# A transformer block on one core: stationary operands of the 256-column products moved by 64 bytes

## The chip, the core and the metric

The kernel runs on one core of one Trainium2 chip. The metric is the device time of one execution in microseconds; the kernel before has three such times. One further execution was recorded by the hardware profiler, and every row shown here is from that one.

On a core, PE (TensorE) multiplies: a *stationary* operand of 128 columns is loaded into the array by a weight load (PEld in the profile), then a *moving* operand of up to 512 columns is streamed past it. Both are read from the on-chip memory SBUF, and the product is written to a PSUM bank. DVE (VectorE) and ACT (ScalarE) do elementwise work, POOL (GpSimd) a little of it, and SP issues most of the transfers from main memory.

## The reference

One block over 512 tokens of width 1024, with a memory of 256 tokens:

```python
def reference(x, mem, ...):
    mix = hybrid_mixer(x, ...)                    # 4 gated-recurrence heads, 4 mLSTM heads
    x = layer_norm(ALPHA * x + mix, ln1_g, ln1_b)
    ca = memory_cross_attention(x, mem, ca_wq, ca_wkv, ca_wo)
    x = layer_norm(ALPHA * x + ca, ln2_g, ln2_b)
    ff = conv_ffn(x, ffn_w_up, ffn_conv_w, ffn_conv_b, ffn_w_down)
    return layer_norm(ALPHA * x + ff, ln3_g, ln3_b)

def memory_cross_attention(x, mem, wq, wkv, wo):
    q = (x @ wq).reshape(bsz, s, CA_HEADS, CA_DH)           # 512 tokens, 4 heads of 256
    k, v = jnp.split(mem @ wkv, 2, axis=-1)                 # 256 memory tokens
    sc = einsum('bshd,bmhd->bhsm', q, k) * CA_DH ** -0.5
    o = einsum('bhsm,bmhd->bshd', softmax(sc), v).reshape(bsz, s, d)
    return o @ wo

def conv_ffn(x, w_up, conv_w, conv_b, w_down):              # 1024 -> 2 x 2816 -> 1024
    gate, val = jnp.split(causal_dwconv(x @ w_up, conv_w, conv_b), 2, axis=-1)
    return (gelu(gate) * val) @ w_down
```

All arrays are float32.

## The kernel before

**Products.** Every float32 operand of a large product is kept as two parts of type fp32r: a rounded part (names ending in h) and the rest (names ending in l). ACT makes the first by a cast, DVE the second by a subtraction: `split` (lines 124 and 125) for weights, `split_evict` (lines 243 and 244) for results that leave PSUM. `mm3` (lines 154 to 156) then issues three products for one: high by high, high by low, low by high. Its first argument after the PSUM bank is the high part of the stationary operand, and each of the three products has a weight load of its own.

**Two shapes of loop.** `col_tile` takes a weight block of 128 columns as stationary operand and streams activations past it. `slab` takes 128 tokens of activations as stationary operand and streams 512 columns of weights. Most products therefore have 512 moving columns. Those with 256 are: the keys (`col_units` over `ca_wkv`, 8 units, the memory's 256 tokens moving), the first two units of the up-projection (`up_units`, computed in two halves of 256 tokens so that the first half can start before the last layer-normalized block is there), the scores in `attend` (queries stationary, keys moving), the products with the values in `pv` (values stationary, probabilities moving), and the last token block of the down-projection, which `slab` cuts into two halves of 256 weight columns (`halves=True`).

**Where operands lie.** Pools hand out buffers per tag, in rotation. Weights come from main memory into `raw` (three buffers of 8192 bytes in each partition), their parts go to `wh` and `wl` (four buffers of 4096 bytes each). Large activations have tag X (`X8`, ten buffers of 8192 bytes); later ones have tag H in a pool that comes after. Small unused tiles (`WP_PAD` and its like) fill up the pools in front. In the built program each buffer of `raw`, `wh`, `wl`, X and H begins at a multiple of 128 bytes within the partition, the slices that products take from them are 512 bytes or a multiple of that apart, and so every fp32r operand of a product begins at a multiple of 128 bytes. The first `wh` buffer lies 256 bytes past a multiple of 512, and the X buffers at multiples of 512. An operand that begins elsewhere is `vaug` (64 bytes past a multiple of 128, and from there in steps of 4 bytes from head to head), a moving operand of float32 products.

**Order.** The engines run their instructions in the order in which they were issued, and the planner of the language has laid out that order from the program text (only the first stage is written by hand). PE goes through the stages one after the other; transposes (lines 252, 417 and 748) stand between the products where their inputs were expected to be ready.

Of the kernel before, what the change touches and what calls it, by code (L numbers as in the profile page):

```python
# [10 lines left out]
F32R = mybir.dt.float32r  # L11
# [6 lines left out]
P = 128  # L18
# [3 lines left out]
KT = D // P  # L22
# [7 lines left out]
QSCALE = P ** -0.5  # L30
CSCALE = 256 ** -0.5
WARM = 7

HEAD = ((0, 1), (1, 1), (2, 2), (4, 2), (6, 2))
CONST_PAD, WP_PAD, SM_PAD = 40, 64, 16
# [4 lines left out]
def hybrid_block_kernel(  # L40
# [28 lines left out]
    wp = ctx.enter_context(tc.tile_pool(name="wp", bufs=1))  # L69
    xp = ctx.enter_context(tc.tile_pool(name="xp", bufs=1))  # L70
# [4 lines left out]
    def mm_bank():  # L75
        return pm.tile([P, 512], F32, name="mm", tag="mm", bufs=5)

    def mx_bank():
        return pm.tile([P, 512], F32, name="mx", tag="mx", bufs=3)

    def X8(dt, name):
        return xp.tile([P, 2048], dt, name=name, tag="X", bufs=10)

    def small(n, name, bufs=4):
        return sm.tile([P, n], F32, name=name, tag=name, bufs=bufs)
# [10 lines left out]
    def f32(t):  # L96
        return t.bitcast(F32)
# [12 lines left out]
    def load_raw(src_list, shape):  # L110
        r = wp.tile([P, 2048], F32, name="raw", tag="raw", bufs=3)
        a, c = shape
        rv = r.rearrange("p (a c) -> p a c", a=a)
        for dst, src in src_list(rv):
            nc.sync.dma_start(dst, src)
        return rv

    def split(src, shape):
        h = wp.tile([P, 1024], F32R, name="wh", tag="wh", bufs=4)
        l = wp.tile([P, 1024], F32R, name="wl", tag="wl", bufs=4)  # L120
        a, c = shape
        hv = h.rearrange("p (a c) -> p a c", a=a)
        lv = l.rearrange("p (a c) -> p a c", a=a)
        A.copy(hv, src)  # L124
        V.tensor_sub(lv, src, f32(hv))  # L125
        return hv, lv

    def slab_units(w, c0, nk):

        k, per = 0, 4  # L130
        while k < nk:
            n = min(4, nk - k)
            raw = load_raw(
                lambda rv, k=k, n=n: [(rv[:, j:min(j + per, n), :],
                                       w[(k + j) * P:(k + min(j + per, n)) * P, c0:c0 + 512]
                                       .rearrange("(k p) c -> p k c", p=P)) for j in range(0, n, per)],
                (4, 512))
            for u in range(0, n, 2):
                h, l = split(raw[:, u:u + 2, :], (2, 512))
                yield k + u, 2, h, l  # L140
            k += n

    def col_units(w, c0, n):

        for j in range(0, n, 2):
            raw = load_raw(
                lambda rv, j=j: [(rv, w[:, c0 + j * P:c0 + (j + 2) * P]
                                  .rearrange("(k p) c -> p k c", p=P))], (8, 256))
            for i in range(2):
                h, l = split(raw[:, :, i * P:(i + 1) * P], (8, P))  # L150
                yield j + i, h, l

    def mm3(ps, ah, al, bh, bl, first, last):
        T.matmul(ps, ah, bh, start=first, stop=False, skip_group_check=True)  # L154
        T.matmul(ps, ah, bl, start=False, stop=False, skip_group_check=True)  # L155
        T.matmul(ps, al, bh, start=False, stop=last, skip_group_check=True)  # L156
# [41 lines left out]
    def col_tile(ps, h, l, xh, xl):  # L198
        for k in range(KT):
            mm3(ps, h[:, k, :], l[:, k, :], xh(k), xl(k), k == 0, k == KT - 1)  # L200
# [7 lines left out]
    wps = mx_bank()  # L208
    for _ in range(WARM):
        T.matmul(wps[:, 0:P], warm, warm, start=True, stop=True)  # L210
# [31 lines left out]
    def split_evict(ps, h, l):  # L242
        A.copy(h, ps)
        V.tensor_sub(l, ps, f32(h))
# [14 lines left out]
    def kslice(ts_, k, c0=0, n=S):  # L259
        o = (k % 4) * 512 + c0  # L260
        return ts_[k // 4][:, o:o + n]

    xTh = [X8(F32R, "xTh") for _ in range(2)]
    xTl = [X8(F32R, "xTl") for _ in range(2)]
    tok = lambda ts_: (lambda k, b: kslice(ts_, k, b * P, P))
    feat = lambda ts_: (lambda k: kslice(ts_, k))
# [4 lines left out]

    binb = q1p.tile([P, 512], F32, name="binb", tag="binb", bufs=2)
    hv = X8(F32, "hv").rearrange("p (b c) -> p b c", b=NB)
    ps = [mm_bank() for _ in range(NB)]

    with tc.manual_schedule(engines={mybir.EngineType.PE, mybir.EngineType.Activation, mybir.EngineType.DVE}):
        for (k0, n), xr, wr in zip(HEAD, xraw, raw0):
            h = wp.tile([P, 1024], F32R, name="wh", tag="wh", bufs=4).rearrange("p (a c) -> p a c", a=2)
            l = wp.tile([P, 1024], F32R, name="wl", tag="wl", bufs=4).rearrange("p (a c) -> p a c", a=2)
            xk = lambda ts_: ts_[k0 // 4].rearrange("p (a c) -> p a c", a=4)[:, k0 % 4:k0 % 4 + n, :]  # L280
            A.copy(h[:, 0:n, :], wr[:, 0:n, :])
            V.tensor_copy(xk(xTh), xr[:, 0:n, :])  # L282
            V.tensor_sub(l[:, 0:n, :], wr[:, 0:n, :], f32(h[:, 0:n, :]))  # L283
            V.tensor_sub(xk(xTl), xr[:, 0:n, :], f32(xk(xTh)))  # L284
            for b in range(NB):
                for i in range(n):
                    k = k0 + i
                    mm3(ps[b], kslice(xTh, k, b * P, P), kslice(xTl, k, b * P, P), h[:, i, :], l[:, i, :],
                        k == 0, k == KT - 1)
# [29 lines left out]

    wif = wp.tile([P, KT, 8], F32, name="wif")  # L320
    nc.sync.dma_start(wif, w_in0[:, MI:MI + 8].rearrange("(k p) c -> p k c", p=P))
    wifh = wp.tile([P, 1024], F32R, name="wh", tag="wh", bufs=4).rearrange("p (k c) -> p k c", k=KT)
    G.memset(f32(wifh), 0.0)
    for j in range(2):
        src = wif[:, :, 4 * j:4 * j + 4]
# [56 lines left out]
    for i, h, l in col_units(w_in0, HF, 4):  # L382
        ps = mm_bank()
        col_tile(ps, h, l, feat(xTh), feat(xTl))
        lf, kin = tt("lf"), tt("kin")
        A.activation(lf, ps, AF.Sigmoid, bias=col(BIN + 4 + i))
        A.activation(kin, ps, AF.Sigmoid, bias=nbin[:, 4 + i:5 + i], scale=-1.0)
        V.tensor_scalar(kin, kin, oml[:, i:i + 1], None, op0=OP.mult)
        lfs[i], kins[i] = lf, kin
    qs = {}  # L390
    for i, h, l in col_units(w_in0, HQ, 4):
        ps = mm_bank()
        col_tile(ps, h, l, feat(xTh), feat(xTl))
        q = tt("q")
        A.activation(q, ps, AF.Sigmoid, bias=col(BIN + i))
        V.scalar_tensor_tensor(q, ps, col(BIN + i), q, op0=OP.add, op1=OP.mult)
        qs[i] = q
# [142 lines left out]
    for base, sc in ((MK, 1.0), (MQ, QSCALE)):  # L540
        for i, h, l in col_units(w_in0, base, 4):
            ps = mm_bank()
            col_tile(ps, h, l, feat(xTh), feat(xTl))
            kq[base, i] = conv_silu(ps, i + (4 if base == MK else 0), sc)
# [78 lines left out]
    mtok = lambda t: (lambda k, b: t[:, k * 256 + b * P:k * 256 + (b + 1) * P])  # L623
    wkv = ca_wkv[0]
    kmh, kml = X8(F32R, "kmh"), X8(F32R, "kml")
    for i, h, l in col_units(wkv, 0, KT):
        if i % 2 == 0:
            ps = mm_bank()
        col_tile(ps[:, (i % 2) * 256:(i % 2 + 1) * 256], h, l, mcols(mTh), mcols(mTl))
        if i % 2 == 1:  # L630
            s = slice((i - 1) * 256, (i + 1) * 256)
            split_evict(ps, kmh[:, s], kml[:, s])
# [63 lines left out]
    x1_last = slab(tok(yTh), tok(yTl), w_out[0], 512, KT, ln1_evict, late=4)  # L696


    vmh, vml = (X8(F32R, n).rearrange("p (b c) -> p b c", b=2) for n in ("vmh", "vml"))

    def v_slab(j, mid=None):
        slab(mtok(mTh), mtok(mTl), wkv, D + j * 512, KT,
# [3 lines left out]
    v_slab(0, x1_last)  # L706


    qmh = [X8(F32R, "qmh") for _ in range(2)]
    qml = [X8(F32R, "qml") for _ in range(2)]  # L710
    for i, h, l in col_units(ca_wq[0], 0, KT):
        ps = mm_bank()
        col_tile(ps, h, l, feat(x1h), feat(x1l))
# [90 lines left out]
        A.copy(kslice(hTh, i), g)  # L804
        V.tensor_sub(kslice(hTl, i), g, f32(kslice(hTh, i)))

    def up_units(i):
        raw = load_raw(lambda rv: [(rv[:, :, j * P:(j + 1) * P],
                                    ffn_w_up[0][:, j * DFF + i * P:j * DFF + (i + 1) * P]
                                    .rearrange("(k p) c -> p k c", p=P)) for j in range(2)], (8, 256))  # L810
        return [split(raw[:, :, j * P:(j + 1) * P], (8, P)) for j in range(2)]

    early = 2
    units = [up_units(i) for i in range(early)]
    banks = [[mm_bank(), mm_bank()] for i in range(early)]
    for half in range(2):
        c0 = half * 256
        for i in range(early):
            for j in range(2):
                if (half, i, j) == (0, 1, 1):  # L820
                    x2_last()
                h, l = units[i][j]
# [31 lines left out]
def build(shapes):  # L854
    import concourse.bacc as _bacc

    nc = _bacc.Bacc("TRN2", target_bir_lowering=False, num_devices=1, dynamic_dma_scratch_size=1024)
    args = [nc.dram_tensor(f"in_{n}_dram", shapes[n], F32, kind="ExternalInput").ap() for n in _INS]
    args.append(nc.dram_tensor("out_0_dram", (1, S, D), F32, kind="ExternalOutput").ap())
    with tile.TileContext(nc) as tc:  # L860
        hybrid_block_kernel(tc, *args)
    return nc
# [19 lines left out]
```

## Time and profile before

| | |
|---|---|
| three executions | 819.33, 821.69 and 823.42 us, median 821.69 |
| the profiled execution's own time | 819.77 us |
| its span, first to last instruction | 818.1 us |
| PE busy | 801.5 us, 98% of the span |
| weight loads (PEld) busy | 674.0 us, 82% |
| DVE, ACT busy | 504.9 us (62%), 318.8 us (39%) |
| granted TensorE clock, mean | 0.995 of full |

In a page row such as `L154 PE MATMUL mm<-x2h,wh 128*128 128x512 f32`, the first name after the arrow is the moving operand and the second the stationary one; 128*128 is the stationary shape, 128x512 the product. The duration of a product is not what it costs in a stream, since products overlap in the array; what one costs is the distance from its start to the next one's. A weight load for the next product runs under the current one.

### The profile page before, as it was taken

The page shows a single profiled execution, that of the slowest core. Times are in us where ns is not written, and L with a number is a line of the kernel's source. Part 1 is how long each engine was busy: PE and PEld are TensorE (multiplying, and loading weights), DVE is VectorE, ACT ScalarE, POOL GpSimd, SP SyncE. Part 2 cuts the span into 40 slices and gives each one's busy share as a digit, 9 for nine tenths or more (in the row PEclk, how much of TensorE's full clock was granted, in tenths as well). Part 3 has the DMA queues.
Part 4 walks back from the last instruction along what each step waited for, and adds up shares of the span by engine and source line. Part 5 has one row for each costly group of instructions (what it writes and reads, how often), then busy time and mean ns, then how long its engine had stood idle before and what let it go on. Part 6 is the DMA issues. An engine that isn't in the chain of part 4 may idle for free.

```text
span 818.1 us, 10034 instructions
## 1 busy us (share of the span) xinstructions
PE 801.5 (98%) x4000; PEld 674.0 (82%) x4000; DVE 504.9 (62%) x863; ACT 318.8 (39%) x434; POOL 30.2 (4%) x52
## 2 busy tenths in 40 slices
PE   8989999999999999999999999999999999999996
PEld 6868887777789888888988988888888888888885
DVE  6563397899787488348548676665566556224237
ACT  3289553353344225237413354444444444222110
POOL 2000100100200010000001000000000000000001
PEclk9999999999999999999999999999999999999998
DMA  8726423135119316321311552223333322142102
GB/s 268 199 72 184 119 79 55 52 81 177 65 52 340 124 52 224 106 84 52 102 58 47 156 154 82 87 89 103 103 104 103 103 99 77 57 154 82 48 1 103
DMA packets 86263, 87.86 MB, mean 107 GB/s; under 512 B 3140, under 2 KB 65732, under 8 KB 86216
## 3 DMA queue, kind: packets, MB, share of 16 engines
q1 hardware_dynamic: 85632, 84.58, 33.6%
q10 hardware_dynamic: 584, 2.64, 0.9%
q8 instruction: 31, 0.51, 0.2%
q14 instruction: 16, 0.13, 0.1%
HBM read 85.10 MB, written 2.12 MB: 107 GB/s over the span
## 4 chain that ended last, share of the span: by engine, by line
PE 88%; DVE 5%; DMA 4%; POOL 1%; issue 1%; ACT 0%; SPq 0%; DVEq 0%; ACTq 0%; POOLq 0%
PE mm L154 27%; PE mm L155 27%; PE mm L156 27%; DMA raw<-in_w_in_dram 3%; PE mx L574 1%; DMA binb<-in_b_in_dram 1%; PE mx L586 1%; PE mx L252 1%; PE mx L464 1%; POOL ss L423 1%; DMA raw<-in_x_t_dram 1%; PE mx L465 1%; PE mx L154 0%; DVE wl L125 0%; PE mx L156 0%
## 5 line engine op out<-in xcount | busy, mean ns | idle before, releaser
L125 DVE TENSOR_TENSOR wl<-raw,wh 128x1024 fp32r<-128x1024 f32 x134 | 163.2, 1221 | 230.3 <-ACT wh L124 229.7
L124 ACT CAST wh<-raw 128x1024 fp32r<-128x1024 f32 x134 | 140.7, 1052 | 242.8 <-PE mm L156 133.0
L154 PE MATMUL mm<-x2h,wh 128*128 128x512 f32 (+1 forms) x384 | 142.8, 372 | 0.0
L155 PE MATMUL mm<-x2l,wh 128*128 128x512 f32 (+1 forms) x384 | 142.6, 371 | 0.0
L156 PE MATMUL mm<-x2h,wl 128*128 128x512 f32 (+1 forms) x384 | 142.6, 371 | 0.0
L155 PEld LDWEIGHTS mm<-x2l,wh 128*128 128x128 f32 x384 | 72.4, 188 | 12.5
L156 PEld LDWEIGHTS mm<-x2h,wl 128*128 128x128 f32 x384 | 72.4, 188 | 12.5
L154 PEld LDWEIGHTS mm<-x2h,wh 128*128 128x128 f32 x384 | 72.4, 188 | 12.3
L155 PE MATMUL mm<-wl,hTh 128*128 128x512 f32 (+1 forms) x198 | 72.4, 366 | 0.0
L154 PE MATMUL mm<-wh,hTh 128*128 128x512 f32 (+1 forms) x198 | 72.4, 366 | 0.0
L795 DVE SCALAR_TENSOR_TENSOR fc<-mm,cols,fc 128x511 f32<-128x511 f32 x88 | 65.6, 746 | 1.5
L156 PE MATMUL mm<-wh,hTl 128*128 128x512 f32 (+1 forms) x180 | 65.8, 365 | 0.0
L154 PE MATMUL mm<-wh,xTh 128*128 128x512 f32 x128 | 51.5, 402 | 0.8 <-DVE xTh L282 0.8
L155 PE MATMUL mm<-wl,xTh 128*128 128x512 f32 x128 | 51.2, 400 | 0.6 <-DVE wl L283 0.5
L156 PE MATMUL mm<-wh,xTl 128*128 128x512 f32 x128 | 50.8, 397 | 0.7 <-DVE xTl L284 0.6
L156 PE MATMUL mm<-xTh,wl 128*128 128x512 f32 x128 | 51.1, 399 | 0.0
L154 PE MATMUL mm<-xTh,wh 128*128 128x512 f32 x128 | 51.1, 399 | 0.0
L155 PE MATMUL mm<-xTl,wh 128*128 128x512 f32 x128 | 51.0, 398 | 0.0
L154 PEld LDWEIGHTS mm<-wh,hTh 128*128 128x128 f32 x198 | 37.4, 189 | 6.2
L155 PEld LDWEIGHTS mm<-wl,hTh 128*128 128x128 f32 x198 | 37.4, 189 | 6.1
L156 PEld LDWEIGHTS mm<-wh,hTl 128*128 128x128 f32 x180 | 33.9, 189 | 5.4
L804 ACT CAST hTh<-fc 128x512 fp32r<-128x512 f32 x22 | 13.7, 620 | 55.7 <-DVE fc L803 55.7
(265 smaller groups left out, 1387.9 us busy)
## 6 DMA issues: line engine op xcount, KB each, us to landing
raw<-in_ffn_w_up_dram SPq DMA_DIRECT2D x44, 512.0 KB, 4.8
raw<-in_w_in_dram SPq DMA_DIRECT2D x14, 1024.0 KB, 8.5
raw<-in_ffn_w_down_dram SPq DMA_DIRECT2D x10, 1024.0 KB, 4.8
raw<-in_ca_wkv_dram SPq DMA_DIRECT2D x8, 1024.0 KB, 5.9
raw<-in_w_out_dram SPq DMA_DIRECT2D x4, 1024.0 KB, 8.8
raw<-in_ca_wq_dram SPq DMA_DIRECT2D x4, 1024.0 KB, 5.4
raw<-in_ca_wo_dram SPq DMA_DIRECT2D x4, 1024.0 KB, 4.9
wt<-scr ACTq DMA_DIRECT2D x4, 640.0 KB, 4.0
```

The lines of the kernel that those rows point to most:

```text
L124: A.copy(hv, src)
L125: V.tensor_sub(lv, src, f32(hv))
L154: T.matmul(ps, ah, bh, start=first, stop=False, skip_group_check=True)
L155: T.matmul(ps, ah, bl, start=False, stop=False, skip_group_check=True)
L156: T.matmul(ps, al, bh, start=False, stop=last, skip_group_check=True)
L252: T.transpose(ps[:, i * P:(i + 1) * P], src[:, k * P:(k + 1) * P], ident)
L423: G.tensor_tensor(out_, out_, neghalf[:, 0:n], op=OP.pow)
L464: T.matmul(at[:, s], ke[:, s], qe[:, s], start=True, stop=True, skip_group_check=True)
L465: T.matmul(at[0:CH, b * P + CH:(b + 1) * P], kxe[:, b, :], qbo[:, b, :], start=True, stop=True, skip_group_check=True)
L574: T.matmul(ps[:, 0:LEN[j]], kT_[:, j * P:(j + 1) * P], qT_[:, j * P:], start=True, stop=True)
L795: V.scalar_tensor_tensor(y[:, s:], ps[:, :S - s], col(FCW + (2 - s) * 44 + ft), y[:, s:], op0=OP.mult, op1=OP.add)
L804: A.copy(kslice(hTh, i), g)
```

## The change

The stationary operands of four of the five groups of 256-column products are moved by 16 elements, that is 64 bytes: the weights of the keys, the weights of the first two up-projection units, the queries and the values. To make room, each buffer of `wh` and `wl` becomes 32 elements (128 bytes) longer and so does each X buffer, whether its tile is moved or not. Tiles that are not moved take the buffer's first elements. The fifth group, the halved last block of the down-projection, has stationary operands that 512-column products use as well; they stay where they are.

```diff
+SKEW = 16
...
-    def X8(dt, name):
-        return xp.tile([P, 2048], dt, name=name, tag="X", bufs=10)
+
+    def X8(dt, name, skew=0):
+        return xp.tile([P, 2080], dt, name=name, tag="X", bufs=10)[:, skew:skew + 2048]
...
-    def split(src, shape):
-        h = wp.tile([P, 1024], F32R, name="wh", tag="wh", bufs=4)
-        l = wp.tile([P, 1024], F32R, name="wl", tag="wl", bufs=4)
+    def split(src, shape, skew=0):
+        h = wp.tile([P, 1056], F32R, name="wh", tag="wh", bufs=4)[:, skew:skew + 1024]
+        l = wp.tile([P, 1056], F32R, name="wl", tag="wl", bufs=4)[:, skew:skew + 1024]
...
-    def col_units(w, c0, n):
+    def col_units(w, c0, n, skew=0):
...
-                h, l = split(raw[:, :, i * P:(i + 1) * P], (8, P))
+                h, l = split(raw[:, :, i * P:(i + 1) * P], (8, P), skew)
...
-    for i, h, l in col_units(wkv, 0, KT):
+    for i, h, l in col_units(wkv, 0, KT, SKEW):
...
-    vmh, vml = (X8(F32R, n).rearrange("p (b c) -> p b c", b=2) for n in ("vmh", "vml"))
+    vmh, vml = (X8(F32R, n, SKEW).rearrange("p (b c) -> p b c", b=2) for n in ("vmh", "vml"))
...
-    qmh = [X8(F32R, "qmh") for _ in range(2)]
-    qml = [X8(F32R, "qml") for _ in range(2)]
+    qmh = [X8(F32R, "qmh", SKEW) for _ in range(2)]
+    qml = [X8(F32R, "qml", SKEW) for _ in range(2)]
...
-    def up_units(i):
+    def up_units(i, skew=0):
...
-        return [split(raw[:, :, j * P:(j + 1) * P], (8, P)) for j in range(2)]
+        return [split(raw[:, :, j * P:(j + 1) * P], (8, P), skew) for j in range(2)]
...
-    units = [up_units(i) for i in range(early)]
+    units = [up_units(i, SKEW) for i in range(early)]
```

Two places that took 1024-element buffers of `wh` and `wl` directly (the hand-ordered first stage and the gates' weights) take the first 1024 of the 1056.

## Rows read from the trace of the kernel before

**Rows 1.** The page: busy time, granted clock in 40 slices, chain that ended last.

```profile
PE 801.5 (98%) x4000; PEld 674.0 (82%) x4000; DVE 504.9 (62%) x863; ACT 318.8 (39%) x434; POOL 30.2 (4%) x52
...
PEclk9999999999999999999999999999999999999998
...
PE 88%; DVE 5%; DMA 4%; POOL 1%; issue 1%; ACT 0%; SPq 0%; DVEq 0%; ACTq 0%; POOLq 0%
```

**Rows 2.** Groups by shape, PE: 256-column products; count, busy us, mean ns.

```profile
L154 PE MATMUL mm<-mTh,wh 128*128 128x256 f32 x64 | 18.7, 292 | 0.0
...
L154 PE MATMUL mm<-x2h,wh 128*128 128x256 f32 x64 | 18.3, 285 | 0.0
...
L155 PE MATMUL mm<-wl,hTh 128*128 128x256 f32 x44 | 12.4, 283 | 0.0
...
L154 PE MATMUL mm<-kmh,qmh 128*128 128x256 f32 x32 | 9.2, 288 | 0.0
...
L154 PE MATMUL mx<-pth,vmh 128*128 128x256 f32 x32 | 9.1, 285 | 0.1
```

**Rows 3.** Timeline of PE, second half of the first up-projection units; start, duration.

```profile
458.28 0.28 PE L155 MATMUL mm<-x2l,wh 128*128 128x256 f32 x1
...
458.87 0.28 PE L154 MATMUL mm<-x2h,wh 128*128 128x256 f32 x1
...
459.35 0.28 PE L155 MATMUL mm<-x2l,wh 128*128 128x256 f32 x1
...
472.43 0.28 PE L156 MATMUL mm<-x2h,wl 128*128 128x256 f32 x1
```

**Rows 4.** Timeline of the weight loads in the same stretch.

```profile
459.35 0.19 PEld L156 LDWEIGHTS mm<-x2h,wl 128*128 128x128 f32 x1
459.47 0.19 PEld L154 LDWEIGHTS mm<-x2h,wh 128*128 128x128 f32 x1
```

**Rows 5.** Windows: 256 columns, then the other up-projection units at 512.

```profile
459.35:472.55 13.20, 13.20 (x113) 13.20 (x111) 7.54 (x10) 7.38 (x9) 0.00 (x0) 1.00 0.41 135
472.55:690.17 217.62, 217.62 (x962) 180.25 (x961) 134.85 (x163) 94.84 (x123) 0.00 (x0) 1.00 0.33 99
```

**Rows 6.** Groups by shape, weight loads: count, busy us, mean ns.

```profile
L154 PEld LDWEIGHTS mm<-mTh,wh 128*128 128x128 f32 x64 | 12.3, 192 | 0.0
...
L154 PEld LDWEIGHTS mm<-x1h,wh 128*128 128x128 f32 x64 | 12.0, 188 | 2.5
...
L464 PEld LDWEIGHTS mx<-ee 128*128 128x128 f32 x32 | 5.0, 188 | 1.6 <-DVE ee L442 0.5
...
L465 PEld LDWEIGHTS mx<-xo 128*64 128x64 f32 x32 | 3.1, 134 | 2.1 <-issue 0.2
```

**Rows 7.** The chain in order of time: eight transposes; four float32 passes.

```profile
378.74 0.87 PE mx L748 x8
...
118.41 0.45 PE mx L489 x4
```

**Rows 8.** Line 124, ACT's cast of weights: what its idle time waited for (us, times).

```profile
  PE mm L156: 133.0, 42
  PE mm L155: 79.7, 63
```

**Rows 9.** Timelines around the last transposes of the second layer normalization.

```profile
455.86 1.40 DVE L673 SCALAR_TENSOR_TENSOR xres<-xres,lnrs,lnb 128x512 f32<-128x512 f32 x2
...
457.29 1.04 PE L252 MATMUL mx<-ident,xres 128*128 128x128 f32 x8
```

**Rows 10.** Timelines of PE and DVE in the products with the values.

```profile
391.94 0.28 PE L156 MATMUL mx<-pth,vml 128*128 128x256 f32 x1
392.29 0.36 PE L154 MATMUL mx<-pth,vmh 128*128 128x256 f32 x1
...
391.72 0.76 DVE L244 TENSOR_TENSOR ptl<-mx,pth 128x256 fp32r<-128x256 f32 x2 [0.62 <-ACT pth L243]
```

**Rows 11.** Lines 523 and 404, DVE's writes: duration ns min/median/max.

```profile
L523 DVE TENSOR_TENSOR vaug<-mm,binb x4: 669/676/680, 140.5 to 144.6; 128x512 f32<-128x512 f32 x4
...
L404 DVE TENSOR_TENSOR hgu<-mm,binb x4: 680/682/691, 101.3 to 106.8; 128x512 f32<-128x512 f32 x4
```

More of the change, by code (lines that the diff above doesn't have):

```diff
@@ L277, in hybrid_block_kernel @@
         for (k0, n), xr, wr in zip(HEAD, xraw, raw0):
-            h = wp.tile([P, 1024], F32R, name="wh", tag="wh", bufs=4).rearrange("p (a c) -> p a c", a=2)
-            l = wp.tile([P, 1024], F32R, name="wl", tag="wl", bufs=4).rearrange("p (a c) -> p a c", a=2)
+            h = wp.tile([P, 1056], F32R, name="wh", tag="wh", bufs=4)[:, 0:1024].rearrange("p (a c) -> p a c", a=2)
+            l = wp.tile([P, 1056], F32R, name="wl", tag="wl", bufs=4)[:, 0:1024].rearrange("p (a c) -> p a c", a=2)
             xk = lambda ts_: ts_[k0 // 4].rearrange("p (a c) -> p a c", a=4)[:, k0 % 4:k0 % 4 + n, :]
@@ L321, in hybrid_block_kernel @@
     nc.sync.dma_start(wif, w_in0[:, MI:MI + 8].rearrange("(k p) c -> p k c", p=P))
-    wifh = wp.tile([P, 1024], F32R, name="wh", tag="wh", bufs=4).rearrange("p (k c) -> p k c", k=KT)
+    wifh = wp.tile([P, 1056], F32R, name="wh", tag="wh", bufs=4)[:, 0:1024].rearrange("p (k c) -> p k c", k=KT)
     G.memset(f32(wifh), 0.0)
```

## The prediction

> **What bounds the kernel now.** I read the page first. PE is busy for 98% of the span, holds 88% of the chain that ended last, and the granted clock is at its upper level, 2.4 GHz, throughout [rows 1]. So time saved on PE is time saved, unless another engine is only just ahead of it.
>
> Next the groups by shape, to count what the change touches [rows 2]. The row shown for each group is one of mm3's three lines. Keys: 3 x 64 = 192 products; first up-projection units: 192; scores: 3 x 32 = 96; products with the values: 96. That is 576 products. The halves of the last down-projection block, with hTh stationary, also have 256 columns, and are not moved: they are the control.
>
> Then the timelines, for the distance from start to start. From 459.35 to 472.43 us there are 109 products, so one costs 13.08 / 109 = 0.120 us [rows 3]. In the 512-column stretch, 960 products share 217.62 us, 226.7 ns each [rows 5]. The difference between the two shapes is 106.7 ns for 256 more columns, which is 2.4 columns a ns: at that clock a column a cycle. So streaming costs 106.7 and 213.3 ns, and both shapes pay 13.3 ns on top. The change can only pay through these 13.3 ns, or add to them.
>
> What are they? The weight load of the next product starts with each product, at 459.35 beside a product at 459.35 [rows 3, 4]. With 256 columns the load takes up the whole distance: PEld is busy 13.20 of 13.20 us, while with 512 it has 17% of the time free [rows 5]. Two rows hint that the two reads of SBUF disturb each other. The loads under 256-column keys last 192 ns on average and those under 512-column products 188 [rows 6]. And the same up-projection product, with the same operands, costs 118 ns in the first five distances after a pause (458.28 to 458.87) and 120 later, with nothing waited for [rows 3]. A fixed price of the instruction would not change like that.
>
> **The change part by part.** *Instructions.* None is added, removed or reordered in the text. Each product, load, cast and subtraction has the same shape as before; only start addresses differ, and the pools grow by 8 x 128 + 10 x 128 = 2304 bytes a partition. Transfers land in raw, which is neither longer nor moved. *The casts and subtractions that write the moved tiles.* I price them at nothing: DVE wrote vaug, whose rows begin 64 bytes off and in steps of 4 bytes, in 676 ns, and an operation of the same shape into an aligned tile took 682 [rows 11]. ACT has no such row; were its casts slower, they would be hidden, as ACT's idle time before them is spent on waiting for PE to release buffers, 133.0 + 79.7 us [rows 8]. *The moved stationary operands.* No row shows an fp32r stationary operand anywhere but at a multiple of 128 bytes, so the price has to be bounded.
>
> Lower bound of the cost: eight transposes, each with a full load of 128 columns, follow each other in 0.87 us, 109 ns each, and four float32 passes in 0.45 us, 112 ns each [rows 7]. So loads of that size can be had every 109 ns. If the move undid all disturbance, a 256-column product would cost 109: 120 - 109 = 11 ns x 576 = 6.3 us saved. Upper bound: if a shifted row made the load read 64 bytes, that is 16 columns, more. A load of 64 columns lasts 134 ns, one of 128 columns 188 [rows 6], so a column costs 54 / 64 = 0.84 ns and 16 of them 13.5 ns; loads are end to end here, so all of it shows: 13.5 x 576 = 7.8 us lost. Between lies nothing, 0.
>
> I take a partial gain. The row of the same product at 118 and the two rows at 109 and 112 are all below 120, and none with 256 columns in a steady stream is above; the middle of 118 and 109 is 113.5, so 6.5 ns x 576 = 3.7 us.
>
> Two rules of the Trainium skill speak against any gain. The page TensorE: Matmul & The Clock Gate (section Step-by-step: what each phase is for) says that the loads have a read port of their own, so that loading the next operand takes nothing from the running product. The page SBUF — State Buffer (section Specifications (TRN2)) puts the memory's lines at 16 bytes, and a shift of 64 is a whole number of these, so that a load would touch as many lines as before. By either, the sum would be 0 instead of -3.7 us. The loads of 192 and 188 ns are the only thing in the trace that speaks against the first; no row bears on the second.
>
> *What is given back.* Where PE already runs level with another engine, a faster product only waits. At 457.29 PE begins the transposes of the last normalized block, and DVE ends that block's normalization at 455.86 + 1.40 = 457.26 [rows 9]. Ahead of them stand 72 moved products, which would end 72 x 6.5 = 0.47 us earlier. The second four transposes need DVE's last piece and would stand at 457.29 + 0.44 - 0.47 = 457.26: nothing is lost at 6.5 ns, and 0.3 us at 11. In the products with the values PE starts at 392.29, 0.23 us later than the 120 after 391.94 would make it, upon DVE's piece of ptl [rows 10]; the scores' 96 x 6.5 = 0.6 us could be lost to that, if DVE's chain does not move along. I take 0.5 us in all, and 0.9 at 11 ns. Likeliest sum: -3.7 + 0.5 = -3.2 us.
>
> *The longer buffers.* The 512-column products, some 2,900, are not moved, but distances between their operands change by multiples of 128 bytes. I price this at nothing: scores, with both operands in X (a multiple of 512 apart), and keys, with wh and X (256 past one), both run at 120. A distance of 128 has no row. One ns each way would be 2.9 us, so the range leaves some room for it.
>
> **The rivals.**
>
> *Part of the overhead goes* (forecast): the profiled execution's 819.77 becomes 816.6. That execution was 1.9 us below the median of the three runs, 821.69; against the median it is 818.5 us.
>
> *All of it goes*: 109 ns. 576 x 11 = 6.3, less 0.9: -5.4, so 816.3 us. For it: rows 7. Against: those rows are float32 passes with 128 moving columns, not fp32r at a column a cycle; and the 512-column products, whose loads end long before they do, pay 13.3 ns as well.
>
> *The move does nothing.* The 13.3 ns are the same for both shapes, to the tenth, as if they belonged to the fp32r product and not to the load. Then the time is 821.7. Against: the 118 ns after a pause. The Trainium skill's rule of a separate read port for loads (TensorE: Matmul & The Clock Gate, Step-by-step: what each phase is for) would give this too, by way of reads that never meet; it has this rival's chance.
>
> *The load becomes longer*, and the kernel slower: a stationary row that begins in the middle of a 128-byte stretch costs the load 13.5 ns. It decides as soon as a load needs more than 120 ns from start to start, which is where the 256-column stages already stand [rows 5]. Price +7.8 us, 829.5. Against it stands only that DVE does not mind such rows [rows 11]; PE has none.
>
> **How the numbers follow.** Chances: part of it goes 0.34, all 0.21, nothing 0.28, longer load 0.17. The least that a measurement of this kernel can tell from no change is about 0.5%, 4.1 us. All (5.4 us) is beyond that, and a quarter of the partial cases, those under 112 ns: 0.21 + 0.09 = 0.30 faster. Slower: the longer load but for small sizes of it, 0.15. Same: 0.55. Predicted: 818.5 us. The range reaches from 813.0 (all of it, with a run 2.4 below the median as the lowest of the three was, and some room for the 512-column products) to 824.0 (nothing, with a run like the highest of three, 823.4). That leaves out the longer load and little else, under 2 in 10.
>
> **What would show each step.** In the timeline of the first up-projection units after the change: distances of 109 to 118 ns, loads near 188 instead of 192. The control should still stand at 120 and the 512-column stretch at 226.7. At the transposes after the first 72 products a pause of up to 0.3 us, before the values' second unit one of up to 0.8. Distances of 133 would show the longer load, 120 that nothing moved. The prediction is wrong in kind if the 512-column products change, since then buffer length and not the 64 bytes sets the time, and wrong in size if the four groups do not gain alike.

## The result and the profile after

The changed kernel takes 829.45 us (median of 5 runs, 829.12 to 831.0); the kernel before, on the same chip, 820.36 (5 runs, 819.33 to 823.42). The ratio is 1.0107, with an interval of 1.0084 to 1.0129. The change makes the kernel slower, outside the predicted range. The profiled execution is the slowest of the five, 831.0 us with a span of 829.3: 11.2 more than before (the medians are 9.1 apart).

First the page of the kernel after: busy time, granted clock in 40 slices, chain that ended last. Line numbers are two higher than before, so mm3's three lines are L156 to L158.

```profile
PE 812.4 (98%) x4000; PEld 673.7 (81%) x4000; DVE 505.2 (61%) x863; ACT 318.8 (38%) x434; POOL 30.2 (4%) x52
...
PEclk9999999999999999999999999999999999999998
...
PE 89%; DMA 5%; DVE 4%; POOL 1%; issue 1%; ACT 0%; SPq 0%; DVEq 0%; ACTq 0%; POOLq 0%
```

Against [rows 1] one figure moved: PE is busy 10.9 us longer with the same 4000 matmuls, and that is nearly the span's 11.2. The clock is at the same level, and PEld, DVE and ACT are busy within 0.3 us of before. So nothing new is waited for: products themselves cost more.

Which ones is read from windows of the kernel after (start and end; length; busy time and instructions of PE, PEld, DVE, ACT, POOL; granted clock; DMA share; GB/s). In order of time: the last 96 key products; the 192 query products, which have 512 columns; the last 48 products with the values; 119 products of the first up-projection units' second half; 960 products of the other units, with 512 columns.

```profile
core 0: us, PE busy (x) PEld busy (x) DVE busy (x) ACT busy (x) POOL busy (x), PEclk, DMA share, GB/s
253.98:264.86 10.88, 10.88 (x98) 10.88 (x97) 7.35 (x8) 5.19 (x6) 0.00 (x0) 1.00 1.01 358
323.84:368.48 44.64, 44.64 (x193) 36.19 (x192) 16.37 (x19) 12.32 (x17) 0.00 (x0) 1.00 0.39 136
401.14:406.60 5.46, 5.46 (x51) 5.46 (x49) 2.67 (x5) 2.36 (x4) 0.00 (x0) 1.00 0.65 187
463.05:477.06 14.01, 14.01 (x121) 14.01 (x120) 8.24 (x11) 8.00 (x11) 0.00 (x0) 1.00 0.44 143
477.06:699.74 222.68, 222.68 (x962) 180.56 (x961) 134.95 (x163) 94.93 (x123) 0.00 (x0) 1.00 0.32 97
```

Divide each length by its products. Keys: 10.88 / 96 = 113.3 ns where they had 120. Values: 5.46 / 48 = 113.7. First up-projection units: 14.01 / 119 = 117.7. These are the moved ones and they gained. The stretch of [rows 5], which the change does not mention, has gone from 226.7 to 222.68 / 960 = 232.0 ns, with the clock at 1.00 and every engine's load in it as before. The query products, also unmoved, went from 226.7 (43.52 us for 192 before) to 44.64 / 192 = 232.5.

The weight loads of the kernel after, by shape (count, busy us, mean ns, idle before), answer to [rows 6]:

```profile
L156 PEld LDWEIGHTS mm<-mTh,wh 128*128 128x128 f32 x64 | 12.1, 189 | 0.0
...
L156 PEld LDWEIGHTS mm<-x1h,wh 128*128 128x128 f32 x64 | 12.2, 190 | 2.9
...
L156 PEld LDWEIGHTS mm<-x2h,wh 128*128 128x128 f32 x384 | 72.4, 188 | 14.0
```

Under the keys 192 became 189, and under the query products 188 became 190. The up-projection's loads (the last line; most of them lie under 512 columns) last 188 ns, though its products became 5.3 ns dearer. No load became 13.5 ns longer.

Last the timeline of PE after, in the keys, at the values' second unit and at the transposes:

```profile
253.98 0.28 PE L156 MATMUL mm<-mTh,wh 128*128 128x256 f32 x1
254.10 0.28 PE L157 MATMUL mm<-mTl,wh 128*128 128x256 f32 x1
254.21 0.28 PE L158 MATMUL mm<-mTh,wl 128*128 128x256 f32 x1
...
396.40 0.28 PE L158 MATMUL mx<-pth,vml 128*128 128x256 f32 x1
396.72 0.36 PE L156 MATMUL mx<-pth,vmh 128*128 128x256 f32 x1
...
461.94 0.28 PE L158 MATMUL mm<-x2h,wl 128*128 128x256 f32 x1
462.06 1.04 PE L254 MATMUL mx<-ident,xres 128*128 128x128 f32 x8
```

Starts are 0.11 to 0.12 us apart in the keys. The pause before the values' second unit is 0.32 - 0.12 = 0.20 us, before it was 0.23 [rows 10]. At the transposes there is none: 0.12 us after the last product.

**The account.** The mean distance from start to start (pauses left out) was taken from both timelines for each group of products, and its change multiplied by the group's count. With 512 columns: the mixer's first products 768 x 3.1 = 2.4 us, its output 192 x 4.4 = 0.85, values' projection 96 x 2.8 = 0.27, queries 192 x 5.8 = 1.1, cross-attention's output 192 x 3.9 = 0.75, up-projection 960 x 5.3 = 5.1, down-projection 462 x 4.0 = 1.85: together +12.3 us. With 256 columns: keys 192 x 5.9 = 1.1, first up-projection units 192 x 2 = 0.4, values 0.2, halved last block 0.2: -1.9. The net, 10.4, is most of the span's 11.2.

### The profile page after: what moved, and what is told of

The parts are those of the page before. It is cut to its first block, busy times and chain, and to the rows that moved or that the text cites. A ratio compares the mean times of both kernels' runs of the same rounds, so it can differ in the third digit from the quotient of the medians.

```text
span 829.3 us, 10034 instructions
## 1 busy us (share of the span) xinstructions
PE 812.4 (98%) x4000; PEld 673.7 (81%) x4000; DVE 505.2 (61%) x863; ACT 318.8 (38%) x434; POOL 30.2 (4%) x52
## 4 chain that ended last, share of the span: by engine, by line
PE 89%; DMA 5%; DVE 4%; POOL 1%; issue 1%; ACT 0%; SPq 0%; DVEq 0%; ACTq 0%; POOLq 0%
PE mm L156 27%; PE mm L157 27%; PE mm L158 27%; DMA raw<-in_w_in_dram 3%; PE mx L576 1%; DMA binb<-in_b_in_dram 1%; PE mx L588 1%; PE mx L254 1%; PE mx L466 1%; POOL ss L425 1%; DMA raw<-in_x_t_dram 1%; PE mx L467 0%; DVE wl L127 0%; PE mx L156 0%; PE mx L419 0%
## 5 line engine op out<-in xcount | busy, mean ns | idle before, releaser
L158 PE MATMUL mm<-x2h,wl 128*128 128x512 f32 (+1 forms) x384 | 144.2, 375 | 0.0
L156 PE MATMUL mm<-x2h,wh 128*128 128x512 f32 (+1 forms) x384 | 144.1, 375 | 0.0
L156 PEld LDWEIGHTS mm<-x2h,wh 128*128 128x128 f32 x384 | 72.4, 188 | 14.0
L158 PEld LDWEIGHTS mm<-x2h,wl 128*128 128x128 f32 x384 | 72.1, 188 | 14.0
L156 PE MATMUL mm<-wh,hTh 128*128 128x512 f32 (+1 forms) x198 | 73.0, 369 | 0.0
L158 PE MATMUL mm<-wh,hTl 128*128 128x512 f32 (+1 forms) x180 | 66.1, 367 | 0.0
L156 PE MATMUL mm<-wh,xTh 128*128 128x512 f32 x128 | 52.5, 410 | 0.8 <-DVE xTh L284 0.8
L158 PE MATMUL mm<-wh,xTl 128*128 128x512 f32 x128 | 51.6, 403 | 0.3 <-DVE xTl L286 0.3
L156 PE MATMUL mm<-xTh,wh 128*128 128x512 f32 x128 | 51.4, 402 | 0.0
L158 PE MATMUL mm<-xTh,wl 128*128 128x512 f32 x128 | 51.1, 399 | 0.0
L156 PEld LDWEIGHTS mm<-wh,hTh 128*128 128x128 f32 x198 | 37.2, 188 | 6.7
L158 PEld LDWEIGHTS mm<-wh,hTl 128*128 128x128 f32 x180 | 33.8, 188 | 6.2
## 6 DMA issues: line engine op xcount, KB each, us to landing
raw<-in_w_out_dram SPq DMA_DIRECT2D x4, 1024.0 KB, 10.4
```

## The experiments

**The question.** The unmoved products share only one thing with the edit: their operands lie in buffers that became 128 bytes longer. Each next `wh` and `wl` buffer, and each next X buffer, therefore starts 128 bytes further along modulo 256, and the distance between a stationary and a moving operand, which was a multiple of 256, becomes in the built program an odd multiple of 128 for about half of the unmoved products. The theory: that distance sets what a product costs beyond its columns. The rivals: the 64-byte move itself slows what comes after; it is the buffers' absolute place; or it is the change from one product's operands to the next one's.

**The length without the move.**

```diff
-SKEW = 16
+SKEW = 0
```

> The buffers are longer by 128 bytes as in the changed kernel, but nothing is moved by 64. Theory A (the buffer length, by which starts no longer agree modulo 256, slows the 512-column products): the 512-column up-projection stays at about 232 ns a product, keys go back to 118 to 120; time 830 to 833 us. Rival B (the 64-byte move itself costs, by its loads or by what follows them): 512 columns back at 226.7, keys at 120, time 820.4.

Measured: 831.2 us, ratio 1.0125 (1.0097 to 1.0153). Windows of the last 96 keys and of the 960 up-projection products:

```profile
254.12:265.51 11.39, 11.39 (x98) 11.39 (x97) 7.25 (x8) 5.17 (x6) 0.00 (x0) 1.00 0.98 371
...
477.85:700.53 222.68, 222.68 (x963) 180.72 (x961) 134.98 (x163) 94.68 (x123) 0.00 (x0) 1.00 0.32 97
```

The 960 products take 222.68 us, to the hundredth what they take in the kernel after, with nothing moved by 64 bytes. So the length alone makes the loss. The keys without the move cost 11.39 / 96 = 118.6 ns, so 5.3 of their 6.7 ns came with the move.

**Half of the lengths each.** In the first, X buffers go back to 2048 elements, with queries and values not moved (the upper part of the diff); in the second, `wh` and `wl` go back to 1024, with keys and first up-projection weights not moved (the lower part; the line of `wl` is like that of `wh`).

```diff
-        return xp.tile([P, 2080], dt, name=name, tag="X", bufs=10)[:, skew:skew + 2048]
+        return xp.tile([P, 2048], dt, name=name, tag="X", bufs=10)[:, skew:skew + 2048]
...
-        h = wp.tile([P, 1056], F32R, name="wh", tag="wh", bufs=4)[:, skew:skew + 1024]
+        h = wp.tile([P, 1024], F32R, name="wh", tag="wh", bufs=4)[:, skew:skew + 1024]
```

> Only the weight buffers wh and wl are 128 bytes longer, keys and first up-projection weights are moved by 64; the X buffers have their old length, queries and values are not moved. A: some of the slowing stays (one operand of each 512-column product changes its place modulo 256 from buffer to buffer): 228 to 232 ns, 824 to 830 us; keys near 113. B: 512 columns at 226.7 and only the keys and first up-projection units slower than 120.

> Only the X buffers are 128 bytes longer, queries and values are moved by 64; wh and wl as before. A: 228 to 232 ns with 512 columns, 824 to 830 us; keys at 118 to 120. B: 512 columns at 226.7, scores and products with the values slower than 120. If the weight buffers alone cause it, this one is at 226.7 and 819 us.

Measured: 830.03 us, 1.011 (1.0087 to 1.0133), with longer weight buffers; 827.4 us, 1.0082 (1.006 to 1.0105), with longer X buffers. Windows of the queries and the 960 up-projection products, longer weight buffers first:

```profile
323.84:368.49 44.65, 44.65 (x194) 36.20 (x192) 16.37 (x19) 12.30 (x17) 0.00 (x0) 1.00 0.39 134
476.65:699.86 223.21, 223.21 (x962) 181.09 (x961) 135.20 (x163) 94.94 (x123) 0.00 (x0) 1.00 0.33 97
```

```profile
322.51:366.02 43.51, 43.51 (x193) 36.05 (x192) 16.45 (x19) 12.30 (x17) 0.00 (x0) 1.00 0.40 137
473.89:696.82 222.93, 222.93 (x962) 180.63 (x961) 134.93 (x163) 94.69 (x123) 0.00 (x0) 1.00 0.32 97
```

Either half alone makes most of the loss, and the losses do not add up, as they would if each buffer had a price of its own. The queries tell the halves apart: their activations (x1h, x1l) lie in H buffers, which nothing lengthened, so only the weight buffers' length can change the distance, and only then do they cost 232.6 instead of 226.6 ns. In the up-projection the activations (x2h, x2l) lie in X, and both lengths count.

**Lengths that keep the distance.** The same move of 64 bytes in buffers longer by 512 bytes (weights alone, then X alone: the two parts of the diff) and by 256 bytes (weights alone, 1088 elements); what is not lengthened is not moved. Where X grows, the unused tile `WP_PAD` goes, and `warm` takes part of `cols`, to make room.

```diff
-        h = wp.tile([P, 1056], F32R, name="wh", tag="wh", bufs=4)[:, skew:skew + 1024]
+        h = wp.tile([P, 1152], F32R, name="wh", tag="wh", bufs=4)[:, skew:skew + 1024]
...
-        return xp.tile([P, 2080], dt, name=name, tag="X", bufs=10)[:, skew:skew + 2048]
+        return xp.tile([P, 2176], dt, name=name, tag="X", bufs=10)[:, skew:skew + 2048]
```

> Keys and first up-projection weights are moved by 64, but wh and wl are 512 bytes longer, so that every unmoved start is where it was modulo 512; X as before. A: 512 columns back at 226.7; keys and the first up-projection units at 113.3: 384 x 6.7 = 2.6 us saved, less up to 0.5 given back: 817.8 to 818.5 us, faster than before. B: slower than before, 821 to 826 us. A third case, that any move of the later pools slows the 512-column products: 232 ns, 830 us.

> Queries and values moved by 64, X buffers 512 bytes longer; wh and wl as before, keys and up-projection weights not moved (for room, the warm-up products at the start read the columns tile instead of one of their own, and the pad tile of the weight pool is gone). 512 columns at 226.7, keys and first up-projection units at 120; scores and products with the values near 113, that is 192 x 6.5 = 1.2 us less, of which up to 0.6 is given back where PE waits for the softmax: 819.0 to 820.0 us.

> Keys and first up-projection weights moved by 64 with wh and wl 256 bytes longer (128 in the change, 512 in the run that restored the 512-column products). If 128-odd starts alone cost: 512 columns at 226.7, 819 us. If a step of 256 from one load to the next costs too, as single rows of the run with weights 128 bytes longer hint (230 ns where the next start is 256 away): 227 to 229 ns on average, 820 to 824 us.

Measured: 819.21 us, 0.9988 (0.9976 to 1.0001); 818.62 us, 0.9987 (0.997 to 1.0003); 819.13 us, 0.9986 (0.9971 to 1.0). Windows of the last 96 keys (weights by 512) or 48 values (X by 512) and of the 960 up-projection products:

```profile
253.46:264.34 10.88, 10.88 (x98) 10.88 (x97) 7.35 (x8) 5.17 (x6) 0.00 (x0) 1.00 1.02 380
...
474.10:691.73 217.63, 217.63 (x963) 180.31 (x961) 134.98 (x163) 94.75 (x123) 0.00 (x0) 1.00 0.33 99
```

```profile
396.10:401.54 5.44, 5.44 (x50) 5.44 (x49) 2.77 (x5) 2.36 (x4) 0.00 (x0) 1.00 0.66 191
...
471.65:689.27 217.62, 217.62 (x962) 180.25 (x961) 134.88 (x163) 94.84 (x123) 0.00 (x0) 1.00 0.33 99
```

The move keeps its gain (10.88 / 96 and 5.44 / 48 are both 113.3 ns), and the 512-column products are back at 217.63 / 960 = 226.7. With 256 bytes the up-projection is at 226.7 too, and the keys at 11.30 / 96 = 117.7:

```profile
249.69:260.99 11.30, 11.30 (x98) 11.30 (x97) 7.27 (x8) 5.16 (x6) 0.00 (x0) 1.00 1.02 371
470.69:688.32 217.63, 217.63 (x963) 180.25 (x961) 134.99 (x163) 94.89 (x123) 0.00 (x0) 1.00 0.33 99
```

The gain is read from the stages. None of the three ratios is clear of no change, though the first run was expected to be faster, at 817.8 to 818.5 us.

**A constant distance.** Here and in the next experiment the kernel before is edited. A small tile in front of `wh` shifts all weight buffers by 64 or by 128 bytes, and one behind them fills the shift up to 512 bytes, so that buffer lengths stay and all that comes behind keeps its place modulo 512.

```diff
+    wp.tile([P, 16], F32, name="shift_pad")     # 32 for 128 bytes
...
+    wp.tile([P, 112], F32, name="rest_pad")     # 96 for 128 bytes
```

> The kernel before, but all wh and wl buffers together begin 64 bytes later, at the old distance of 4096 from each other: every product with weights now has one operand 64 bytes past a multiple of 128, the 512-column ones too. No buffer is longer. Theory A in the form 'a constant offset of 64 helps, changing offsets hurt': keys and first up-projection units 113 to 118 ns, 512 columns at or below 226.7, 814 to 819 us. In the form '64 helps 256-column products and hurts those of 512': 512 columns at 230 to 236, 828 to 845 us.

> As the run with all weights 64 bytes later, but 128 bytes: the distance between the two operands of a product is an odd multiple of 128, the same for all weight buffers. If the offset of 128 itself is what costs, the 512-column products stand at 233 to 235 ns throughout, 838 to 843 us. If only the change of offset from buffer to buffer costs, they stand at 226.7 and the time is that of before, 820.

Measured: 831.04 us, 1.0141 (1.0118 to 1.0164), and 833.08 us, 1.0161 (1.0134 to 1.0187). Windows of the last 96 keys and the 960 up-projection products, 64 bytes first (there also the first 282 products of the down-projection):

```profile
252.60:263.48 10.88, 10.88 (x98) 10.88 (x97) 7.32 (x8) 5.17 (x6) 0.00 (x0) 1.00 1.03 370
...
475.69:699.68 223.99, 223.99 (x963) 180.48 (x961) 135.00 (x163) 94.85 (x123) 0.00 (x0) 1.00 0.32 97
699.68:764.24 64.56, 64.56 (x283) 52.96 (x282) 22.50 (x28) 13.84 (x14) 0.00 (x0) 1.00 0.28 90
```

```profile
250.58:261.98 11.40, 11.40 (x99) 11.40 (x97) 7.23 (x7) 5.17 (x6) 0.00 (x0) 1.00 1.01 364
...
475.14:699.14 224.00, 224.00 (x962) 180.19 (x961) 134.97 (x163) 94.74 (x123) 0.00 (x0) 1.00 0.32 96
```

Here every pair of the up-projection has the same distance modulo 256 and nothing varies from buffer to buffer, and its 512-column products cost 223.99 / 960 = 233.3 ns at either shift. So a constant distance is enough for the price; no change from one product to the next is needed. In the down-projection the weights are the moving operand, so that the shift by 64 makes the distance, counted from moving to stationary operand, 192: there a product costs 64.56 / 282 = 228.9 ns. The price of the second run is the one expected, its time is not (838 to 843 us); why it falls short was not traced. The first also shows the two shapes wanting opposite things: 64 bytes bring the 256-column keys to 113.3 and the 512-column products of the up-projection to 233.3.

Where distances are mixed, a product's own distance is not the whole of its price. In the built programs half of the 960 products lie at 0 and half at 128 modulo 256 in the kernel after and with longer weight buffers, a third at 0 and two thirds at 128 with longer X buffers. At 226.7 and 233.3 ns each, the means would be 230.0 and 231.1; measured are 232.0 and 232.5, and 232.2. With the trace's starts sorted by these distances, the products at 0 average 231.1 ns and those at 128 232.8 in the kernel after, 232.7 and 232.0 with longer X buffers. So a product at 0 pays as well when products at 128 run beside it.

**Both operands moved.** `WP_PAD` grows by 64 bytes, and with it the weights, the activations and all that comes behind move by the same 64 bytes.

```diff
-CONST_PAD, WP_PAD, SM_PAD = 40, 64, 16
+CONST_PAD, WP_PAD, SM_PAD = 40, 80, 16
```

> The kernel before with its weight pool and all pools behind it 64 bytes later: both operands of every fp32r product lie 64 bytes past a multiple of 128, their distances from each other are those of before. If the distance of the two operands sets the price: 512 columns at 226.7, 256 columns at 120, time within 0.3% of before. If the place of a stationary operand by itself does: 256 columns at 113 to 118 and 512 columns at 233, 830 us.

Measured: 821.51 us, 1.0019 (1.0005 to 1.0033). Windows of the last 96 keys and the 960 products:

```profile
251.74:263.26 11.52, 11.52 (x98) 11.52 (x97) 6.37 (x7) 5.16 (x6) 0.00 (x0) 1.00 1.00 359
...
473.43:691.06 217.63, 217.63 (x962) 180.28 (x961) 134.89 (x163) 94.76 (x123) 0.00 (x0) 1.00 0.35 99
```

120.0 and 226.7 ns, as before. Where the operands lie costs nothing here; how far apart they lie does. (The 0.2% is the least that one may read from a ratio here, since no product's price changed.)

**A sweep.** This and the last experiment edit the changed kernel again. Weight buffers of 1152 elements, X as before, queries and values not moved, and each unit of the keys and of the later up-projection starts at another offset: `KEYS` and `UPS` list them in elements of 4 bytes. Each up-projection unit has 48 products.

```diff
+KEYS = (0, 4, 8, 12, 16, 24, 32, 48)
+UPS = (0, 4, 8, 12, 16, 20, 24, 28, 32, 36, 40, 48, 56, 64, 72, 80, 96, 112, 120, 128)
...
-                h, l = split(raw[:, :, i * P:(i + 1) * P], (8, P), skew)
+                h, l = split(raw[:, :, i * P:(i + 1) * P], (8, P), KEYS[j + i] if skew else 0)
...
-        u = up_units(i)
+        u = up_units(i, UPS[i - early])
```

> wh and wl 512 bytes longer as in the run that restored the 512-column products, but each unit of the keys and of the later up-projection lies at an offset of its own: keys 0 to 192 bytes, up-projection (512 columns) 0 to 512 bytes, 48 products at each. If the offset modulo 256 sets the price: 512 columns at 226.7 at 0, 256 and 512 bytes and 230 to 235 between, the same at offsets that are 256 apart; 256 columns at 120 at 0 and lowest near 64. If the price repeats at 128, then 128 and 384 give 226.7 as well.

One run, 823.84 us. Windows of the units at 0, 16, 32, 64 bytes, then 128, 192, 224, 256, 288, 384 and 448:

```profile
472.01:482.92 10.91, 10.91 (x51) 9.02 (x49) 8.54 (x11) 5.28 (x9) 0.00 (x0) 1.00 0.48 142
482.92:493.81 10.89, 10.89 (x50) 9.01 (x49) 6.66 (x8) 4.72 (x7) 0.00 (x0) 1.00 0.33 96
493.81:505.00 11.19, 11.19 (x50) 9.02 (x48) 6.66 (x8) 4.70 (x7) 0.00 (x0) 1.00 0.32 94
...
516.20:527.39 11.19, 11.19 (x50) 9.02 (x48) 6.65 (x8) 4.71 (x7) 0.00 (x0) 1.00 0.32 94
...
560.95:572.15 11.20, 11.20 (x50) 9.01 (x48) 6.66 (x8) 4.70 (x7) 0.00 (x0) 1.00 0.33 95
...
594.55:605.54 10.99, 10.99 (x49) 9.02 (x48) 6.65 (x8) 4.70 (x7) 0.00 (x0) 1.00 0.34 98
605.54:616.74 11.20, 11.20 (x50) 9.00 (x48) 6.65 (x8) 4.71 (x7) 0.00 (x0) 1.00 0.33 94
616.74:627.63 10.89, 10.89 (x50) 9.01 (x49) 6.65 (x8) 4.71 (x7) 0.00 (x0) 1.00 0.33 98
627.63:638.82 11.19, 11.19 (x50) 9.02 (x48) 6.66 (x8) 4.70 (x7) 0.00 (x0) 1.00 0.32 94
...
650.01:661.17 11.16, 11.16 (x49) 9.05 (x48) 6.66 (x8) 4.72 (x7) 0.00 (x0) 1.00 0.25 95
661.17:672.17 11.00, 11.00 (x49) 9.02 (x48) 6.66 (x8) 4.71 (x7) 0.00 (x0) 1.00 0.27 95
```

The loads are busy 9.0 us in each; only the time from one product's start to the next changes. The ladder: 10.89 / 48 = 226.9 at 16 bytes, 11.19 / 48 = 233.1 at 32 and 64, 11.00 / 48 = 229.1 at 192, and at 256, 288 and 448 the values of 0, 32 and 192 again. The unit at 384 stands at 11.16 / 48 = 232.5, that at 128 at 233.3. The units not shown lie at 231.7 (80 bytes) to 234.2 (96), but for 512 bytes, where 226.7 came back. So with one distance throughout a unit the price repeats after 256 bytes, to about 1 ns. For 256-column products (the last half of each key unit): 120.0 at 0 and 96, 118.1 at 32, 117.8 at 48 and 192, 113.3 at 64, 118.4 at 128; the unit at 16 stood at about 120 among transposes.

**The whole change with a length that keeps the distance.** Both kinds of buffer are longer by 256 bytes; room is made as for the X buffers above.

```diff
-        h = wp.tile([P, 1056], F32R, name="wh", tag="wh", bufs=4)[:, skew:skew + 1024]
+        h = wp.tile([P, 1088], F32R, name="wh", tag="wh", bufs=4)[:, skew:skew + 1024]
...
-        return xp.tile([P, 2080], dt, name=name, tag="X", bufs=10)[:, skew:skew + 2048]
+        return xp.tile([P, 2112], dt, name=name, tag="X", bufs=10)[:, skew:skew + 2048]
```

> The whole change, with all four groups moved by 64, but with wh, wl and X buffers 256 bytes longer instead of 128 (room made as in the run with X 512 bytes longer). If the distance of the two operands modulo 256 alone sets the disturbance: 512 columns at 226.7, keys, first up-projection units, scores and products with the values at 113 to 118, 815 to 818 us, faster than before by 0.2 to 0.5%. If a step of 256 between the high and low parts (which lie in X buffers of both kinds) costs as well: 512 columns with X operands at 228 to 230, 820 to 824 us.

Measured: 818.65 us (12 runs; the kernel before 820.09, 17 runs), 0.9977 (0.9964 to 0.999). Windows of the last 96 keys, the last 48 values, the 960 products:

```profile
252.60:263.48 10.88, 10.88 (x98) 10.88 (x97) 7.24 (x8) 5.18 (x6) 0.00 (x0) 1.00 1.00 367
397.24:402.68 5.44, 5.44 (x51) 5.44 (x49) 2.77 (x5) 2.36 (x4) 0.00 (x0) 1.00 0.65 190
472.39:690.02 217.63, 217.63 (x963) 180.19 (x962) 134.98 (x163) 94.90 (x123) 0.00 (x0) 1.00 0.33 99
```

This is the version with the lowest ratio, faster than both kernels by it and by the stages, if just above the 815 to 818 us expected; its 0.23% is, however, hardly more than the 0.19% that came without any product's price changed. That the high and low parts lie 256 bytes apart here instead of a multiple of 512 cost the 512-column products nothing: 226.7.

**All runs side by side**, ns per product in the stretches named (960 = later up-projection units, 119 = second half of the first ones):

```
                                  time    keys  queries  first up  960 up  values
                                   us    (256)    (512)     (256)   (512)   (256)
before                           820.36  120.0    226.7     119.9   226.7   120.0
after: both longer by 128        829.45  113.3    232.5     117.7   232.0   113.7
longer by 128, no move           831.2   118.6    232.5     118.4   232.0   119.1
weights longer by 128, moved     830.03  113.3    232.6     114.4   232.5   120.0
X longer by 128, moved           827.4   120.0    226.6     118.8   232.2   113.7
weights longer by 512, moved     819.21  113.3    226.7     117.8   226.7   120.0
weights longer by 256, moved     819.13  117.7    226.7     117.8   226.7   120.0
X longer by 512, moved           818.62  120.0    226.7     119.9   226.7   113.3
both longer by 256, moved        818.65  113.3    226.7     117.8   226.7   113.3
all weights shifted by 64        831.04  113.3    233.3     117.7   233.3   120.0
all weights shifted by 128       833.08  118.8    232.4     118.6   233.3   120.0
both operands shifted by 64      821.51  120.0    226.7     119.9   226.7   120.0
```

## Why the prediction was wrong

*What bounds the kernel*: right. PE's own pace sets the end, and 10.9 us more of PE are 11.2 more of span. That both shapes pay 13.3 ns on top of streaming, and that these ns can move, was right too: they are 6.7 at the best distance seen for 256 columns and 20 at a common bad one for 512 (233.3 - 213.3).

*What the 13.3 ns are*: that the two reads disturb each other is borne out in so far as the price follows their distance and not their place. One of its hints, loads of 192 ns under the keys and 188 under 512 columns, was none, for loads of 192 stood under 512-column products of the mixer before as well:

```profile
L154 PEld LDWEIGHTS mm<-xTh,wh 128*128 128x128 f32 x128 | 24.6, 192 | 4.8
```

Nor does a load's length follow the price: in the sweep the loads of a unit take 9.0 us at 226.9 as at 233.1 ns a product.

*The partial gain*: right for some stretches. 113.5 was forecast; the last 96 keys and the last 48 products with the values gave 113.3 and 113.7 in the kernel after, and 113.3 in the version with 256 bytes. As 113.5 was the middle of 118 and 109, with no row at that distance, the close agreement is in part luck; at the same 64 bytes 117.8 was measured too. The first 48 products with the values average 120.9 in the kernel after. The four groups do not gain alike, though, which the prediction named as a sign of a wrong size: the first up-projection units settle at 117.7, and the scores, whose operands both lie in the lengthened X, average 119.6 in the kernel after. Instead of 3.7 us the moved products gained about 1.7, and 2.5 is the sum in the version with 256 bytes (keys 1.1, first units 0.4, values 0.6, scores 96 x 3.6 ns = 0.35).

*What is given back*: the pauses were priced at 0.5 us in all. Shown are none at the transposes and 0.20 instead of 0.23 before the values' second unit, so nothing was added there.

*Casts and subtractions at nothing*: right; DVE and ACT are busy 505.2 and 318.8 us, before 504.9 and 318.8 [rows 1].

*The longer buffers*: the step that failed. "The 512-column products, some 2,900, are not moved, but distances between their operands change by multiples of 128 bytes. I price this at nothing". The price is up to 6.6 ns a product, 4.3 on the mean (12.3 us over some 2,860), and it is the whole loss: without the move the kernel is as slow, with a length of 256 or 512 bytes it is not slow at all. The sum that was put at -3.2 us became +10.4 by stages, 12.3 lost and 1.9 gained. The text gave the reason to doubt itself: "A distance of 128 has no row", and its two rows were for 256 columns, at distances that are multiples of 256. A multiple of 128 is not the same as one of 256. It also named the sign that came true: the 512-column stretch moved from 226.7 to 232.0, "since then buffer length and not the 64 bytes sets the time".

*The control*, the halved last block, was to stay at 120; it averages 119.6 before and 118.2 after, since its weights lie in the longer buffers too.

*The rivals*. The longer load gave 829.5 us, and 829.45 was measured; this is chance. That rival said 133 ns for the keys and longer loads; the keys cost 113.3 and their loads 189 ns instead of 192. It is refuted, and the number says nothing for it. That the move does nothing is refuted by the same 113.3. All of the overhead, 109 ns, was not reached in any stretch.

The trace does not bear out, for these fp32r products, the rule of the Trainium skill (TensorE: Matmul & The Clock Gate, Step-by-step: what each phase is for) that loading the next operand takes nothing from the running product: with the same instructions, and loads as long, a 512-column product costs 226.7 or 233.3 ns when only the distance between the two operands of all products is another. The Trainium skill's line of 16 bytes (SBUF — State Buffer, Specifications (TRN2)) does not decide either: a shift by one such line cost nothing (226.9), a shift by two did (233.1).

**What stays open.** Why a distance matters, that is, what in the memory the two reads share, was not tried; the runs show the dependence and its period. Two levels also stand side by side unexplained: 113.3 and 117.7 or 117.8 ns for 256 columns with weights at the same offset of 64 bytes. The keys stand at 117.7 with weights alone longer by 256 bytes and at 113.3 with both kinds of buffer longer by 256, and in that version the first up-projection units are at 117.8. So the distance modulo 256 of one pair is not the only thing that counts there. Nor is it in the kernel after, where products at 0 pay as well; how the products beside it come to count is open.

## What to carry to other kernels

A longer buffer moves every later buffer of its pool, so price it for every operand that lies there, first of all for the products that the edit does not name and that are most numerous; a length that keeps the old distances (here a multiple of 256 bytes) makes the same edit harmless. "Nothing" is a price like any other and wants a row at the same distance and shape, or an end in the range as large as the groups concerned: the prediction allowed the moved products 11 ns down and 13.5 up, and the 2,900 others 1 ns. When a total agrees with a rival, look at the stage in which that rival would have to show before believing it.

## What the hardware showed that was not expected

In a stretch where all products have the same distance between their two operands in SBUF, the cost of an fp32r product depends on that distance, and repeats after 256 bytes to about 1 ns: at 512 columns 226.7 ns at 0 and 16 bytes, 229 at 192, 232 to 234 at the others tried; at 256 columns 120.0 at 0 and 113.3 or 117.8 at 64. Where distances of 0 and 128 are mixed, the products at 0 pay too (231.1 ns in the kernel after). The two shapes have their best and worst distances in different places, and no offset tried serves both: 64 bytes for all weights cost 1.4% (1.0118 to 1.0164), while 64 bytes for the 256-column operands alone, distances else kept, gave a ratio of 0.9977, hardly further from 1 than the 1.0019 of the run in which no product's price changed, and 2.5 us by the stages.
